# Two more pairs in seven products, one pair fewer, and the differences in a step of their own

## The chip, the cores and the metric

The kernel runs on one core of a Trainium2 chip. The metric is the device time of one execution in microseconds. Before the change the median of three runs is 991.41 us (990.34 to 991.68).

## The reference

One layer of a hybrid decoder trunk, in fp32, for 256 tokens of width 2048:

```python
h = rmsnorm(x, norm_g)
proj = h @ w_in                                   # 2048 -> 13824 columns
qa, ka, va, ga, qb, kb, vb, gb, xc, gc, mg = jnp.split(proj, cuts, axis=-1)
ya = moba_attention(qa, ka, va, rpe_table)        # 8 heads of 128
yb = swa_attention(qb, kb, vb, sinks, rpe_table)  # 16 query heads of 64, window 128
yc = rglru_branch(xc, conv_w, conv_b, w_r, b_r, w_i, b_i, lam)   # conv, two gates in 8 blocks, recurrence
y = jnp.stack([ya * jax.nn.silu(ga), yb * jax.nn.silu(gb), yc * jax.nn.silu(gc)], axis=2)
y_d = jnp.einsum('bsnc,ncd->bsnd', y, w_br)
merged = jnp.einsum('bsnd,bsnd->bsd', jax.nn.sigmoid(mg), y_d)
x = x + merged @ w_out
x = x + jax.nn.sigmoid(rmsnorm(x, ple_norm_g) @ w_pg) * (p @ w_pp)
return rmsnorm(x, final_norm_g)
```

Nearly all of the work is four matrix products with 256 rows: `w_in`, `w_br`, `w_out`, `w_pg`.

## The kernel before

**Precision.** Each fp32 product is three products of rounded parts: hi x hi, hi x lo and lo x hi (`mm3`, matmuls of lines 185, 186 and 187). Activations are split into hi and lo once. Weights are split as they come: a tile of 128 x 1024 (two K tiles of a chunk of 512 columns) is fetched on SP's queue (`fetch`, L110, five buffers, tiles named `r_...`), cast to the hi part on ACT (`split`, L136, `wh_...`), and the lo part is a subtraction on DVE (L138, `wl_...`). Hi and lo have four buffers each, so a cast must wait until TensorE has finished with the tile four places earlier.

**Staging.** A chunk of 512 output columns is 16 K tiles x 2 halves of the tokens x 3 products = 96 matmuls of 128x512, summed in two PSUM banks (`matrix_psum`, two such tiles). Four more banks (`aux`) serve attention, branch C's gate products and the pairs' single products. When a chunk is done ACT evicts it (L657 `to_features` for q, k and gates, two instructions), DVE transposes blocks of it (`flip_...`, L803), and it goes through DRAM to the feature layout.

The chunks of `w_in` are named by their first row: va, xc (16, 24), gc (32, 40), qa (48, 56), ka (64, 72), ga (80, 88), C's merge gates (96 to 120), kv (128), qb (136, 144), gb (152, 160), A's and B's merge gates (168 to 224). Between them stand the tiles of `w_br` (brc, bra, brb). Branch C's eight pairs of gate products `pg0` to `pg7` (matmuls of 128x256) are handed out among the tiles of the q and k chunks. Each one goes round: matmuls, sigmoid of half r on ACT (`rg`, L715), matmuls, sigmoid of half i (`ig`), and casts of the next block's `cv` and `wr` on ACT (L390) with their lo parts on DVE (L391).

**Pairs in seven products.** `pair_of` (L251) takes two chunks together. Their first four K tiles form a 2 x 2 block matrix, multiplied in seven block products in place of eight, with sums and differences of blocks of weights (DVE, L263) and of activations (`make_sums`, L235). A block product is two K tiles x 3 = 6 matmuls of 128x512. Four products (five, one, six, seven: the heads) need nothing of the chunks' PSUM; `head(left)` starts them inside the chunk ahead, one per weight tile near its end. Seven then puts DVE's sums into the PSUM tile of the first chunk, and the plain tiles of the pair add to it. Three, two and four follow between the pair's own tiles. In the kernel before there are pairs for qb (136), the last two merge gates (216), both halves of w_out, and the first two chunks of w_pg. When a pair is opened, three of its four weight blocks are fetched and the difference t1 = 12 - 11 is made at once on DVE; the second difference, 22 - 12, is made in `five`.

**What sets the order.** The program is written once in Python; a scheduler with its own model of the engines orders every engine's instructions when the kernel is built. Each engine then executes its list in that order. `tc.issue_after` and `tc.high_priority` steer it. SP's list holds the fetches of weights in the order of use, each waiting for a free buffer.

## Time and profile before

| | |
|---|---|
| median of three runs | 991.41 us |
| profiled execution | 988.83 us |
| its span | 987.0 us |
| TensorE (PE) busy | 974.9 us, 99%, 4426 matmuls |
| DVE busy | 712.2 us, 72% |
| ACT busy | 587.6 us, 60% |
| DMA | 232.63 MB, mean 236 GB/s |
| granted TensorE clock | 0.997 |

The profiled execution is 1.83 us longer than its span, and 2.58 us shorter than the median. PE is a row of matmuls, PEld its weight loads, which overlap them. A matmul's recorded duration includes its pipeline, so the distance between two starts says what one costs. A time such as "781.48" is the start in microseconds from the begin of the span. Buffer numbers are left out of names in the profile (`wl_in` is the lo part of any tile of w_in).

### The profile page before, as it was taken

To read this page: it belongs to the slowest core of one execution; us is meant where nothing else is said; L and a number is where in the kernel's file an instruction comes from. 1 tells how busy PE (TensorE), PEld (TensorE's weight loads), DVE (VectorE), ACT (ScalarE), POOL (GpSimd) and SP (SyncE) were. 2 spreads that over 40 slices of the span, in tenths; PEclk is the share of its full clock that TensorE was granted. 3 is DMA by queue.
4 is the path that set the end of the run, shared out by engine and by line. 5 is a ranking of instruction groups with operands and counts; after the bars stand their busy time and mean duration, and the time that the engine had idled before them with its cause. 6 is when DMAs were issued, how large, how long until landed. Compare 5 with 4: busy or idle time off the path is not lost.

```text
span 987.0 us, 12481 instructions
## 1 busy us (share of the span) xinstructions
PE 974.9 (99%) x4426; PEld 810.4 (82%) x4426; DVE 712.2 (72%) x1000; ACT 587.6 (60%) x826; POOL 3.6 (0%) x12
## 2 busy tenths in 40 slices
PE   9999999999999999999999999999999999999996
PEld 7888888888888888888888888888888788878886
DVE  6746875566887676666557888698678589898683
ACT  7644645557676566545556767765555455676662
POOL 0000000000000000000000000000000000000000
PEclk9999999999999999999999999999999999999998
DMA  9867876777777767747788776667747967769752
GB/s 360 322 190 226 285 231 222 226 222 236 234 259 246 218 195 246 221 128 232 246 262 267 235 249 218 220 225 230 258 140 258 347 209 261 219 208 360 254 175 85
DMA packets 83494, 232.63 MB, mean 236 GB/s; under 512 B 9400, under 2 KB 30952, under 8 KB 82920
## 3 DMA queue, kind: packets, MB, share of 16 engines
q1 hardware_dynamic: 76896, 219.32, 68.3%
q10 hardware_dynamic: 6536, 12.52, 3.6%
q8 instruction: 34, 0.56, 0.2%
q14 instruction: 28, 0.23, 0.1%
HBM read 211.06 MB, written 20.75 MB: 235 GB/s over the span
## 4 chain that ended last, share of the span: by engine, by line
PE 88%; DVE 4%; DMA 4%; issue 2%; ACT 1%; SPq 0%; DVEq 0%; ACTq 0%
PE ps_in L186 20%; PE ps_in L187 20%; PE ps_in L185 20%; PE ps_pg L185 3%; PE ps_pg L187 3%; PE ps_pg L186 3%; PE ps_bra L186 1%; PE ps_brc L187 1%; PE ps_bra L187 1%; PE ps_bra L185 1%; PE ps_brc L185 1%; PE ps_brc L186 1%; DMA b_out<-w_out_dram 1%; PE ps_brb L187 1%; PE ps_brb L186 1%
## 5 line engine op out<-in xcount | busy, mean ns | idle before, releaser
L138 DVE TENSOR_TENSOR wl_in<-r_in,wh_in 128x1024 fp32r<-128x1024 f32 x224 | 273.0, 1221 | 148.7 <-ACT wh_in L136 143.5
L136 ACT CAST wh_in<-r_in 128x1024 fp32r<-128x1024 f32 x224 | 234.7, 1051 | 203.7 <-PE ps_in L187 163.3
L186 PE MATMUL ps_in<-wl_in,h 128*128 128x512 f32 x896 | 349.3, 390 | 2.1 <-DVE wl_in L138 2.1
L185 PE MATMUL ps_in<-wh_in,h 128*128 128x512 f32 x896 | 349.3, 390 | 0.0
L187 PE MATMUL ps_in<-wh_in,h 128*128 128x512 f32 x896 | 349.0, 390 | 0.0
L186 PEld LDWEIGHTS ps_in<-wl_in,h 128*128 128x128 f32 x896 | 168.3, 188 | 37.1 <-DVE wl_in L138 3.2
L187 PEld LDWEIGHTS ps_in<-wh_in,h 128*128 128x128 f32 x896 | 168.3, 188 | 34.6
L185 PEld LDWEIGHTS ps_in<-wh_in,h 128*128 128x128 f32 x896 | 168.3, 188 | 34.4
L138 DVE TENSOR_TENSOR wl_pg<-r_pg,wh_pg 128x1024 fp32r<-128x1024 f32 x24 | 29.3, 1222 | 14.3 <-ACT wh_pg L136 14.2
L185 PE MATMUL ps_pg<-wh_pg,x_hi 128*128 128x512 f32 (+1 forms) x104 | 38.9, 374 | 0.3 <-DVE ps_pg L263 0.3
L186 PE MATMUL ps_pg<-wl_pg,x_hi 128*128 128x512 f32 (+1 forms) x104 | 38.8, 373 | 0.0
L187 PE MATMUL ps_pg<-wh_pg,x_lo 128*128 128x512 f32 (+1 forms) x104 | 38.8, 373 | 0.0
L186 PE MATMUL ps_out<-wl_out,m_hi 128*128 128x512 f32 x96 | 37.5, 391 | 0.0
L187 PE MATMUL ps_out<-wh_out,m_lo 128*128 128x512 f32 x96 | 37.4, 389 | 0.0
L185 PE MATMUL ps_out<-wh_out,m_hi 128*128 128x512 f32 x96 | 37.2, 390 | 0.0
L136 ACT CAST wh_out<-r_out 128x1024 fp32r<-128x1024 f32 x24 | 25.2, 1052 | 16.8 <-PE ps_out L187 6.5
L136 ACT CAST wh_pg<-r_pg 128x1024 fp32r<-128x1024 f32 x24 | 25.1, 1051 | 13.9 <-PE ps_pg L187 9.8
L138 DVE TENSOR_TENSOR wl_brc<-r_brc,wh_brc 128x1024 fp32r<-128x1024 f32 x16 | 19.6, 1223 | 19.0 <-ACT wh_brc L136 19.0
L136 ACT CAST wh_brc<-r_brc 128x1024 fp32r<-128x1024 f32 x16 | 16.9, 1055 | 25.1 <-PE ps_in L187 25.1
L138 DVE TENSOR_TENSOR wl_out<-r_out,wh_out 128x1024 fp32r<-128x1024 f32 x24 | 29.1, 1217 | 3.3 <-ACT wh_out L136 3.3
L136 ACT CAST wh_brb<-r_brb 128x1024 fp32r<-128x1024 f32 x16 | 16.9, 1054 | 19.6 <-DMA r_brb<-w_br_dram 6.6
L138 DVE TENSOR_TENSOR wl_brb<-r_brb,wh_brb 128x1024 fp32r<-128x1024 f32 x16 | 19.5, 1221 | 8.8 <-ACT wh_brb L136 8.7
(409 smaller groups left out, 1400.7 us busy)
## 6 DMA issues: line engine op xcount, KB each, us to landing
r_in<-w_in_dram SPq DMA_DIRECT2D x228, 512.0 KB, 4.4
r_pg<-w_pg_dram SPq DMA_DIRECT2D x30, 512.0 KB, 4.8
r_out<-w_out_dram SPq DMA_DIRECT2D x28, 512.0 KB, 4.9
r_brc<-w_br_dram SPq DMA_DIRECT2D x16, 512.0 KB, 3.6
r_bra<-w_br_dram SPq DMA_DIRECT2D x16, 512.0 KB, 5.0
r_brb<-w_br_dram SPq DMA_DIRECT2D x16, 512.0 KB, 4.0
d_b<-flip_b SPq DMA_DIRECT2D x32, 96.0 KB, 2.7
turn_b<-d_b SPq DMA_DIRECT2D x8, 384.0 KB, 4.9
```

The lines of the kernel that those rows point to most:

```text
L136: casts.append(nc.scalar.copy(hi[:, c], r[:, c]).ins)
L138: los.append(nc.vector.tensor_tensor(lo[:, c], r[:, c], hi[:, c].bitcast(F32), op=ALU.subtract).ins)
L185: nc.tensor.matmul(ps, ah, bh, start=first, stop=False, **more)
L186: nc.tensor.matmul(ps, ah, bl, start=False, stop=False, **more)
L187: nc.tensor.matmul(ps, al, bh, start=False, stop=last, **more)
```

## The change

1. The two differences of a pair become a step of their own, `differ`, which is the first of now five heads. It stands behind the lo part that was issued last.
2. A pair may be `inside`: products five, one and six use the two banks of its own first PSUM tile, and only seven takes an `aux` bank.
3. Two pairs are added, both `inside`: ka (rows 64 to 79), opened after qa's first chunk, with its heads in qa's second chunk; and gb (152 to 167), opened ahead of the qb pair, with its heads in the second half of the qb pair. The host packs their columns accordingly.
4. The pair of w_pg becomes two plain chunks: K tiles 0 to 11 of both, then 12 to 15 of each. The activation sums of x for that pair go.
5. In branch B's merge, the heads of the next pair start two tiles before the end of chunk 0 or 2 of `w_br` (`beyond`). The sums of the merged activations get a higher priority.

The core of the diff:

```diff
     def head(left):
-        while coming and len(coming) >= left - 1:
+        while coming and len(coming) >= left + beyond[0] - 1:
             coming.pop(0)()
...
-            if alone:
+            if alone and inside and n != 7:
+                if not pss:
+                    pss.append(matrix_psum(f"{name}_0"))
+                dst = pss[0][:, int(n == 5)]
+            elif alone:
                 dst = aux(f"m{n}_{name}")
...
+        def differ():
+            raw["t1"] = temp(f"t1_{name}").rearrange("p k t -> p (k t)")
+            z.update({0: raw["t1"][:, :CW], 1: raw["12"][:, :CW], 2: raw["t1"][:, CW:], 3: raw["12"][:, CW:]})
+            with tc.issue_after(los[-1]):
+                on_vector(raw["t1"], raw["12"], raw["11"], ALU.subtract)
+                on_vector(raw["12"], raw["22"], raw["12"], ALU.subtract)
+
         def five():
-            on_vector(raw["12"], raw["22"], raw["12"], ALU.subtract)
             ms[5] = product(5, sum_of(0), "t1")
...
-        heads = [five, one, six, seven]
+        heads = [differ, five, one, six, seven]
...
-        raw["t1"] = temp(f"t1_{name}").rearrange("p k t -> p (k t)")
-        z.update({0: raw["t1"][:, :CW], 1: raw["12"][:, :CW], 2: raw["t1"][:, CW:], 3: raw["12"][:, CW:]})
-        on_vector(raw["t1"], raw["12"], raw["11"], ALU.subtract)
         return lambda: coming.extend(heads), rest
...
-        for c in range(2):
-            turned_q(c, in_chunk())
+        turned_q(0, in_chunk())
+        open_ka, ka_pair = in_pair(1, True)
+        open_ka()
+        turned_q(1, in_chunk())
...
-        for c in range(2):
-            turned_k(c, in_chunk())
+        ka_pair(turned_k)
...
+        open_gb, gb_pair = in_pair(2, True)
+        open_gb()
         qb_pair(features(qT, rs_q[DB], "qb"))
...
-        for c in range(2):
-            silu(chunk(g, c), f"gb{c}")
+        gb_pair(lambda c, ps: silu(chunk(g, c), f"gb{c}", ps))
...
-            if (bi, n) in ((2, 1), (2, 3)):
-                pairs[0][0]()
+            if bi == 2:
+                beyond[0] = 4 if n % 2 == 0 else 0
+                if n % 2 == 0:
+                    pairs[0][0]()
...
-    pairs.pop(0)[1](KD - 4, gated)
+    pss = [matrix_psum(f"pg{i}").rearrange("p h c -> p (h c)") for i in range(2)]
+    gets = [weights_of(w_pg, i * KD * CW // WT, f"pg{i}", WT // CW) for i in range(2)]
+    for last in (False, True):
+        for i in range(2):
+            for k in range(KD - 4, KD) if last else range(KD - 4):
...
+                    mm3(pss[i][:, h * CW : (h + 1) * CW], [t[:, h * P : (h + 1) * P] for t in act_of(*x2T)[k]],
+                        [t[:, c] for t in w], k == 0, k == KD - 1)
+            if last:
+                gated(i, pss[i].rearrange("p (h c) -> p h c", h=NH))
```

The built order shows it at three places. In names, the number behind the last underscore counts buffers; `in56_7` is weight tile 7 of the chunk at row 56, and `in64_0_6` in a pair is the tile of chunk 0 that starts at K tile 6. Line numbers of the changed kernel are 2 to 23 higher than before (L136 and L138 excepted).

TensorE, where qa's second chunk (in56) ends and ka (in64) begins. Before, pg5's matmuls stand among ka's first tile:

```order
L185 MATMUL ps_in64_1744<-wh_in64_0_1747,h0_109 128x512
L186 MATMUL ps_in64_1744<-wl_in64_0_1748,h0_109 128x512
L185 MATMUL pg5_1372<-cv5_1373,wr5_1376 128x256
L187 MATMUL ps_in64_1744<-wh_in64_0_1747,h0_109 128x512
L185 MATMUL ps_in64_1744<-wh_in64_0_1747,h0_109 128x512
L186 MATMUL pg5_1372<-cv5_1373,wr5_1376 128x256
L187 MATMUL pg5_1372<-cv5_1373,wr5_1376 128x256
L186 MATMUL ps_in64_1744<-wl_in64_0_1748,h0_109 128x512
```

Now in56 is followed by pg5, pg6 (six matmuls each) and one matmul of pg7, and these by product seven, the rest of pg7 and the first plain tile:

```order
L185 MATMUL pg7_1414<-cv7_1415,wr7_1418 128x256
L185 MATMUL m7_in64_1740<-wh_in64_m7_1741,sum_h_824 128x512
L186 MATMUL m7_in64_1740<-wl_in64_m7_1742,sum_h_824 128x512
L187 MATMUL m7_in64_1740<-wh_in64_m7_1741,sum_h_824 128x512
L185 MATMUL m7_in64_1740<-wh_in64_m7_1741,sum_h_824 128x512
L186 MATMUL m7_in64_1740<-wl_in64_m7_1742,sum_h_824 128x512
L187 MATMUL m7_in64_1740<-wh_in64_m7_1741,sum_h_824 128x512
L186 MATMUL pg7_1414<-cv7_1415,wr7_1418 128x256
L187 MATMUL pg7_1414<-cv7_1415,wr7_1418 128x256
L185 MATMUL ps_in64_0_1652<-wh_in64_0_4_1803,h1_110 128x512
```

On ACT at that place now stand the cast of in64_0_6 (its buffer is in56_7's), the evictions of qa's second chunk and the sigmoids and casts of pg5 to pg7 in a row:

```order
L136 CAST wh_in64_0_6_1831<-r_in64_0_6_1829 128x1024
L667 ACTIVATE qa_1431<-ps_in56_1594,rs_q128_575 128x4x128 x2
L725 ACTIVATE rg_587<-pg5_1372,vecs_84 128x256
L269 COPY ps_in64_1_1865<-t1_in64_1631 128x512
L725 ACTIVATE ig_588<-pg5_1372,vecs_84 128x256
L400 CAST cv6_1394<-cv_585 128x256
L400 CAST wr6_1397<-wri_586 128x256
L725 ACTIVATE rg_587<-pg6_1393,vecs_84 128x256
L725 ACTIVATE ig_588<-pg6_1393,vecs_84 128x256
L400 CAST cv7_1415<-cv_585 128x256
L400 CAST wr7_1418<-wri_586 128x256
```

So the gate products stand together where they stood apart.

ACT, where the first chunk of the qb pair (in136_0) ends. Before, four tiles of the second chunk (in136_1) are cast ahead of the evictions of qb:

```order
L136 CAST wh_in136_1_4_3958<-r_in136_1_4_3956 128x1024
L136 CAST wh_in136_1_6_3976<-r_in136_1_6_3974 128x1024
L136 CAST wh_in136_1_8_3994<-r_in136_1_8_3992 128x1024
L136 CAST wh_in136_1_10_4012<-r_in136_1_10_4010 128x1024
L657 ACTIVATE qb_3582<-ps_in136_0_3749,rs_q64_576 128x4x128 x2
L136 CAST wh_in136_1_12_4030<-r_in136_1_12_4028 128x1024
```

Now one is, and behind the evictions they alternate with the products of gb (in152), the first of which is t1:

```order
L136 CAST wh_in136_1_4_3985<-r_in136_1_4_3983 128x1024
L667 ACTIVATE qb_3601<-ps_in136_0_3768,rs_q64_576 128x4x128 x2
L136 CAST wh_in152_m5_4002<-t1_in152_3980 128x1024
L136 CAST wh_in136_1_6_4014<-r_in136_1_6_4012 128x1024
L136 CAST wh_in152_m1_4030<-b_in152_3821 128x1024
L136 CAST wh_in136_1_8_4044<-r_in136_1_8_4042 128x1024
```

On DVE t1 stands behind the flip of qb's first chunk:

```order
L138 TENSOR_TENSOR wl_in136_1_4_3986<-r_in136_1_4_3983,wh_in136_1_4_3985 128x1024
L813 STREAM_TRANSPOSE flip_qb0_3972<-qb_3601 128x8x4x32
L265 TENSOR_TENSOR t1_in152_3980<-b_in152_3821 128x1024
L265 TENSOR_TENSOR b_in152_3821<-r_in152_22_3824,b_in152_3821 128x1024
L138 TENSOR_TENSOR wl_in152_m5_4003<-t1_in152_3980,wh_in152_m5_4002 128x1024
L138 TENSOR_TENSOR wl_in136_1_6_4015<-r_in136_1_6_4012,wh_in136_1_6_4014 128x1024
```

DVE, where the last pair of merge gates (in216) ends and chunk 2 of `w_br` for branch B (brb2) begins. Before, t1 of the out0 pair stands ahead of the last lo part of in216:

```order
L263 TENSOR_TENSOR t1_out0_6594<-b_out0_6589 128x1024
L138 TENSOR_TENSOR wl_in216_1_14_6572<-r_in216_1_14_6569,wh_in216_1_14_6571 128x1024
L263 TENSOR_TENSOR b_out0_6589<-r_out0_22_6592,b_out0_6589 128x1024
L138 TENSOR_TENSOR wl_brb2_0_6600<-r_brb2_0_6597,wh_brb2_0_6599 128x1024
L138 TENSOR_TENSOR wl_brb2_1_6618<-r_brb2_1_6615,wh_brb2_1_6617 128x1024
L138 TENSOR_TENSOR wl_brb2_2_6636<-r_brb2_2_6633,wh_brb2_2_6635 128x1024
```

Now both differences stand behind the lo part of brb2_1:

```order
L138 TENSOR_TENSOR wl_in216_1_14_6610<-r_in216_1_14_6607,wh_in216_1_14_6609 128x1024
L138 TENSOR_TENSOR wl_brb2_0_6636<-r_brb2_0_6633,wh_brb2_0_6635 128x1024
L138 TENSOR_TENSOR wl_brb2_1_6654<-r_brb2_1_6651,wh_brb2_1_6653 128x1024
L265 TENSOR_TENSOR t1_out0_6669<-b_out0_6627 128x1024
L265 TENSOR_TENSOR b_out0_6627<-r_out0_22_6630,b_out0_6627 128x1024
L138 TENSOR_TENSOR wl_brb2_2_6675<-r_brb2_2_6672,wh_brb2_2_6674 128x1024
```

They moved by three lo parts.

## The prediction

> **What bounds the kernel now.** I read the page first: busy times, then the costliest groups.

> ```profile
> span 987.0 us, 12481 instructions
> PE 974.9 (99%) x4426; PEld 810.4 (82%) x4426; DVE 712.2 (72%) x1000; ACT 587.6 (60%) x826; POOL 3.6 (0%) x12
> L138 DVE TENSOR_TENSOR wl_in<-r_in,wh_in 128x1024 fp32r<-128x1024 f32 x224 | 273.0, 1221 | 148.7 <-ACT wh_in L136 143.5
> L136 ACT CAST wh_in<-r_in 128x1024 fp32r<-128x1024 f32 x224 | 234.7, 1051 | 203.7 <-PE ps_in L187 163.3
> L186 PE MATMUL ps_in<-wl_in,h 128*128 128x512 f32 x896 | 349.3, 390 | 2.1 <-DVE wl_in L138 2.1
> ```

> TensorE is busy for nearly the whole span. So time can come from two places only: fewer matmuls, or fewer and shorter waits of TensorE. ACT and DVE have room on average, but their casts and low-part subtractions are released by TensorE itself (ACT waits mostly for `ps_in` L187, the end of an older tile). The splits therefore run only a few tiles ahead.

> Next, the waits of TensorE, all of them:

> ```profile
> PE ps_in L186 <- DVE wl_in L138: 2.1, 2, 1.6
> PE m_pg L185 <- ACT sum_x L247: 0.8, 1, 0.8
> PE busy L452 <- PEq L1262: 0.8, 1, 0.8
> PE ps_pg L185 <- DVE ps_pg L263: 0.3, 1, 0.3
> ```

> Apart from the start, three waits are there to be removed: 1.6 us on a low part of `w_in`, 0.8 and 0.3 us in the w_pg pair. Everything beyond that must come out of the count of matmuls.

> A matmul's recorded 390 ns is not its price, as the starts show:

> ```profile
> 782.51 0.39 PE L187 MATMUL ps_in<-wh_in,h 128*128 128x512 f32 x1
> 782.75 0.39 PE L185 MATMUL ps_in<-wh_in,h 128*128 128x512 f32 x1
> 782.97 0.39 PE L186 MATMUL ps_in<-wl_in,h 128*128 128x512 f32 x1
> ```

> One starts 0.23 us after the other (0.227 over long runs of such rows). That is what a matmul of 128x512 costs here.

> **The change part by part: the matmuls.** A pair saves one of eight block products, 2 K-halves x 3 = 6 matmuls, 6 x 0.227 = 1.36 us. Two pairs are added (ka, gb), one goes (w_pg): net -1.36 us.

> **The w_pg pair's waits.** Both rows above (`m_pg`, `ps_pg`) go with the pair. Recorded idle is 0.83 and 0.30; by starts, which also lose the overlap of 0.16 at the end of an idle piece, it is 0.99 and 0.47. Sum: -1.46. In the new code the K tiles 12 to 15 are asked for only after 144 matmuls of the first two chunks, 144 x 0.227 = 33 us, so I see nothing that takes the place of these waits.

> **The differences of the out0 pair.** The largest wait comes from here:

> ```profile
> 779.06 1.23 DVE L263 TENSOR_TENSOR t_out<-b_out 128x1024 f32<-128x1024 f32 x1 [7.48 <-DMA b_out<-w_out_dram]
> 780.21 1.22 DVE L138 TENSOR_TENSOR wl_in<-r_in,wh_in 128x1024 fp32r<-128x1024 f32 x1
> 781.34 1.22 DVE L263 TENSOR_TENSOR b_out<-r_out,b_out 128x1024 f32<-128x1024 f32 x1
> 782.48 1.22 DVE L138 TENSOR_TENSOR wl_brb<-r_brb,wh_brb 128x1024 fp32r<-128x1024 f32 x1
> 785.34 1.23 DVE L138 TENSOR_TENSOR wl_brb<-r_brb,wh_brb 128x1024 fp32r<-128x1024 f32 x1 [1.65 <-ACT wh_brb L136]
> 781.48 0.50 PE L186 MATMUL ps_in<-wl_in,h 128*128 128x512 f32 x1 [1.58 <-DVE wl_in L138]
> 780.59 1.04 ACT L136 CAST wh_brb<-r_brb 128x1024 fp32r<-128x1024 f32 x1 [2.94 <-DMA r_brb<-w_br_dram]
> 784.26 1.05 ACT L136 CAST wh_brb<-r_brb 128x1024 fp32r<-128x1024 f32 x1 [2.63 <-DMA r_brb<-w_br_dram]
> ```

> DVE stood 7.48 us in front of t1 until the block of w_out landed, with the low part of the last in216 tile queued behind it; TensorE waited 1.74 us by starts (to 781.48). In the new order t1 and the second difference stand behind the low parts of tiles 0 and 1 of brb2. The tile of in216 is freed. But what is late next is in the same fence: ACT waited for the DMA of tile 0 to 780.59 and of tile 1 to 784.26, and neither load changes its place on SP's queue. Tile 1's low part then still ends near 786.6. Had TensorE gone on at 779.74 without a wait, it would ask for this one at 779.74 + 24 x 0.227 = 785.2: it waits 1.4 us there. Behind it on DVE now stand the two differences (2 x 1.14 between starts) before tile 2's low part: that ends at 790.0, asked for at 786.6 + 12 x 0.227 = 789.3, 0.7 us more. Together 2.1 against 1.74 before. I take 0 for this place; the bounds are -1.74 (the loads come earlier too) and +0.7.

> **The ka pair at the end of qa chunk 1 (in56).** Before, TensorE had plain tiles of ka to run while branch C's recurrent-gate products (pg5 to pg7) went back and forth with ACT and DVE:

> ```profile
> 202.51 0.28 PE L185 MATMUL pg<-cv,wr 128*128 128x256 f32 x1
> 202.62 0.28 PE L186 MATMUL pg<-cv,wr 128*128 128x256 f32 x1
> 202.74 0.28 PE L187 MATMUL pg<-cv,wr 128*128 128x256 f32 x1
> 203.06 0.47 ACT L715 ACTIVATE ig<-pg,vecs 128x256 f32<-128x256 f32 x1 [0.67 <-PE pg L187]
> 203.44 0.40 ACT L390 CAST cv<-cv 128x256 fp32r<-128x256 f32 x1
> 203.57 0.42 DVE L718 TENSOR_TENSOR ig<-ig,cv 128x256 f32<-128x256 f32 x1
> 203.73 0.41 ACT L390 CAST wr<-wri 128x256 fp32r<-128x256 f32 x1
> 203.91 0.42 DVE L391 TENSOR_TENSOR cv<-cv,cv 128x256 fp32r<-128x256 f32 x1
> 204.25 0.42 DVE L391 TENSOR_TENSOR wr<-wri,wr 128x256 fp32r<-128x256 f32 x1
> ```

> A step from TensorE's last pg matmul (202.74 + 0.28) to its sigmoid and on to the next split's last subtraction (204.25 + 0.42) takes 1.65 us, and nothing waited since plain tiles lay between. In the built order of the change nothing lies between. Behind in56's last matmul stand pg5, pg6 and the first matmul of pg7, 13 in a row, then product seven (m7), the rest of pg7, and then tile in64_0_4, which adds to a PSUM tile that DVE writes only after m7. Everything is a chain, and it starts late, because ACT has a cast that waits for in56's last matmul and both evictions of qa1 ahead of pg5's sigmoid:

> ```profile
> 195.49 1.05 ACT L136 CAST wh_in<-r_in 128x1024 fp32r<-128x1024 f32 x1 [1.67 <-PE ps_in L187]
> 196.44 1.26 ACT L657 ACTIVATE qa<-ps_in,rs_q 128x512 f32<-128x512 f32 x2
> 197.59 0.47 ACT L715 ACTIVATE rg<-pg,vecs 128x256 f32<-128x256 f32 x1
> ```

> With 0 at the end of in56's last matmul: cast to 1.0, evictions to 2.15 (1.15 between starts), sigmoid of pg5 to 2.62 (197.59 less 195.49 is 2.10, the same chain). pg5's second half starts at 2.66 and ends at 3.18; its sigmoid at 3.22, the splits of pg6 1.61 later (203.06 to 204.67) at 4.83. pg6's last matmul of the first half starts at 4.87, ends 5.15, sigmoid to 5.66, second half 5.70 to 6.22, sigmoid at 6.26; cast of wr7 7.34. pg7's first matmul 7.38, m7 from 7.50, its last matmul starts at 8.63 and ends at 9.02. Then DVE's sum into PSUM:

> ```profile
> L263 DVE TENSOR_TENSOR ps_in<-b_in,m_in x2: 689/692/696, 446.9 to 741.2; 128x512 f32<-128x512 f32 x2
> L263 DVE TENSOR_TENSOR t_in<-b_in x2: 1216/1218/1221, 412.5 to 702.6; 128x1024 f32<-128x1024 f32 x2
> L267 ACT COPY ps_in<-b_in 128x512 f32<-128x512 f32 x4 | 2.3, 586 | 1.4 <-DVE b_in L263 1.4
> ```

> 0.69 from 9.06: tile in64_0_4 starts at about 9.78. TensorE's own work in that time is 15 pg matmuls at 0.117 (202.51 to 202.74 is two) and 6 at 0.227, 3.12 us. **Wait: 6.7 us.** The copy of 0.59 between pg5's two sigmoids and the flip of qa on DVE fit in the chain's own gaps. Bounds: 5.2 if the cast (0.95) and one eviction (0.58) get ahead, 8.0 if the copy (0.59) and half the flip (0.7) fall into the chain.

> **The gb pair at the end of qb chunk 0 (in136).** Here the differences are the new step. On DVE it stands behind the flip of qb0, which needs both evictions, and ACT's next casts stand behind it: first m5 of the gb pair (which is t1), then in136_1_6. Before, four tiles of chunk 1 were cast ahead of the evictions; now one.

> ```profile
> 473.63 1.26 ACT L657 ACTIVATE qb<-ps_in,rs_q 128x512 f32<-128x512 f32 x2
> 474.92 1.25 DVE L803 STREAM_TRANSPOSE flip_qb<-qb 128x1024 f32<-128x1024 f32 x1
> ```

> From in136_0_14's last matmul: evictions to 1.36 (0.1 for the start), flip from 1.4, t1 from 2.58 (starts 1.15 apart, as 780.21 to 781.34) to 3.8, cast of m5 to 4.88, its low part to 6.17. TensorE has tile in136_1_4 (12 matmuls), one of m5 and one of in136_1_6: 14 x 0.227 = 3.18 us, and goes on at 6.2. **Wait: 3.0 us.** Nothing waits behind it: in136_1_6's low part ends at 7.3, when m5's other five matmuls do. Bounds: 1.8 if DVE could take t1 before the flip, 4.0 if a load or another cast comes between.

> **The sum.** 988.83 (profiled execution, 1.83 around the span) - 1.36 - 1.46 + 0 + 6.7 + 3.0 = 995.7. The runs' median, 991.41, lies 2.58 above that execution, so **998.2 us**, 0.7% slower. DVE's extra work for a pair (seven rows of 1.22, three of them low parts of the added products, and four sums of 0.69, some 11 us) I cost at nothing: DVE is 28% idle, and its low parts end 1 to 3 us before they are asked for at the other places; without this cover each would cost up to its length.

> [...] TensorE's clock stayed full across the largest wait of before:

> ```profile
> 780.00:784.00 4.00, 2.52 (x11) 2.10 (x12) 3.69 (x4) 1.04 (x1) 0.00 (x0) 1.00 1.03 410
> ```

> (seventh value, the granted clock: 1.00 with 2.52 of 4 us busy). [...]

> **The rivals.**
> *Neither wait comes.* If pg5 to pg7 get through while TensorE is still busy and t1 is early, the change does what it says: 998.2 - 9.7 = 988.5, or 986.8 with the out0 wait gone as well. For it: the before trace hides exactly these chains at no cost. Against: TensorE takes its matmuls in the order built, and that order has no plain tile there. It decides from the point where the two new waits sum to less than 2.8 us, what is saved elsewhere.
> *One of the two.* Only the ka wait: 995.2. Only the gb wait: 991.5, no change. For it: they are 270 us apart and have different causes.
> *The clock falls.* At half speed for as long after each wait as it lasted (6.7 and 3.0 us), half of that is lost: 4.8 us, 1003. Against: the window row above.

> **How the numbers follow.** Both waits 62%, with its own range 994.5 to 1001; ka's alone 11%; gb's alone 6%; neither 10%; the clock 6%; further waits, where I took DVE's additions as hidden, 5%. About 0.2% (2 us) is what a measurement here can tell from no change. Slower: 62 + 11 + 6 + 5 = 84%. Same: 6%. Faster: 10%. The range, 991 to 1002, leaves out the faster case and the clock, some 2 in 10 at most.

> **What would show it.** In the profile after: a TensorE wait on ACT's sigmoids and casts and on DVE's `cv`/`wr` near 197 to 206 us, summing to 6 to 7 us, in groups named pg; a wait of `ps_in` on the cast and low part of `wl_in_m` near 475 us of about 3 us; no `m_pg` group; near 790 us waits on `wl_brb` in place of `wl_in`. TensorE's count 6 lower and its waits some 10 us larger would make each step right. If pg matmuls alternate with `ps_in` ones near 200 us, the main term is wrong.

## The result

The changed kernel takes 1005.84 us (median of four runs, 1005.45 to 1007.01). The kernel before, run beside it, takes 990.90 us (990.34 to 991.68). The ratio is 1.0148, with a 95% interval of 1.0133 to 1.0164: the change makes the kernel 1.5% slower. The forecast was 998.2 us, slower by 0.7%. The side was right; the size was not, and the time lies outside the range of 991 to 1002.

The profiled executions differ by more than the medians do: 18.2 us of span (1005.2 less 987.0). The one of before was 2.1 us under its median, the one of after (1007.01) 1.2 us above. The account below is made between the two profiled executions.

The page of the changed kernel, its head and the granted clock by slices:

```profile
span 1005.2 us, 12487 instructions
PE 982.8 (98%) x4420; PEld 814.2 (81%) x4420; DVE 720.6 (72%) x1005; ACT 594.9 (59%) x834; POOL 3.2 (0%) x12
PEclk9999999979999999999999999999999999989999
```

The count of matmuls fell by 6, as it should, and TensorE is still busy for 98% of the span. But its busy time rose by 7.9 us. Fewer matmuls can't do that at the same clock, and the granted clock shows a slice at 7 tenths (201 to 226 us) and one at 8 (880 to 905 us).

All waits of TensorE in the changed kernel behind the first 20 us:

```profile
PE ps_out L185 <- ACT wh_out L136: 2.9, 1, 2.9
PE pg L185 <- ACT rg L725: 2.9, 2, 2.4
PE pg L185 <- ACT wr L400: 2.3, 2, 1.2
PE ps_in L185 <- ACT wh_in_m L136: 2.2, 1, 2.2
PE ps_in L185 <- ACT wh_in L136: 0.8, 2, 0.4
PE ps_out L186 <- DVE wl_out L138: 0.5, 1, 0.5
PE ps_in L185 <- DVE ps_in L265: 0.4, 1, 0.4
```

The rows named `pg` and the last one are the ka place, `wh_in_m` is the gb place; both were forecast. Of the two waits in the row `wh_in`, one belongs to the gb place and one stands at 183 us. `wh_out` and `wl_out` were not: they are a third place, in the second half of w_out. The row `m_pg` of before is gone.

The next rows are stretches of 3.41 us of TensorE's time at the three places (columns: length, then busy time of PE, PEld, DVE, ACT and POOL, the granted clock, DMA share, GB/s). Why 3.41 is told in the last section.

```profile
202.03:205.44 3.41, 0.80 (x5) 0.41 (x3) 2.42 (x3) 3.19 (x6) 0.00 (x0) 1.00 0.57 166
205.44:208.85 3.41, 1.94 (x6) 1.50 (x6) 1.67 (x5) 1.33 (x4) 0.00 (x0) 0.50 0.81 270
208.85:212.27 3.42, 2.26 (x6) 1.71 (x6) 1.10 (x3) 1.07 (x3) 0.00 (x0) 0.50 0.34 68
212.27:215.68 3.41, 3.05 (x9) 2.25 (x8) 2.30 (x3) 1.91 (x3) 0.00 (x0) 0.50 0.29 117
485.33:488.75 3.42, 1.26 (x6) 0.65 (x4) 3.38 (x4) 1.39 (x2) 0.00 (x0) 1.00 0.48 110
488.75:492.16 3.41, 3.03 (x8) 2.25 (x8) 3.41 (x4) 2.50 (x3) 0.00 (x0) 0.50 0.53 155
888.11:891.52 3.41, 1.22 (x6) 0.68 (x4) 0.00 (x0) 0.36 (x1) 0.00 (x0) 1.00 1.01 407
891.52:894.93 3.41, 2.20 (x4) 1.45 (x5) 2.69 (x3) 3.11 (x5) 0.00 (x0) 0.50 0.85 300
894.93:898.35 3.42, 3.42 (x9) 2.64 (x8) 3.15 (x4) 3.42 (x10) 0.00 (x0) 0.50 0.84 287
```

At each place TensorE first waits at full clock, and then goes on at half of it for one to three such stretches (at the ka place with more waits in them). At half clock a matmul of 128x512 starts every 0.427 us instead of 0.227.

The rows behind the two waits that were forecast: at the ka place the cast that heads the chain, pg5's second half and the first plain tile; at the gb place t1, its cast and product five.

```profile
201.94 1.04 ACT L136 CAST wh_in<-r_in 128x1024 fp32r<-128x1024 f32 x1 [1.67 <-PE ps_in L187]
204.57 0.38 PE L185 MATMUL pg<-cv,wr 128*128 128x256 f32 x1 [2.36 <-ACT rg L725]
214.13 0.79 PE L185 MATMUL ps_in<-wh_in,h 128*128 128x512 f32 x1 [0.36 <-DVE ps_in L265]
```
```profile
486.08 1.18 DVE L265 TENSOR_TENSOR t_in<-b_in 128x1024 f32<-128x1024 f32 x1
487.36 1.05 ACT L136 CAST wh_in_m<-t_in 128x1024 fp32r<-128x1024 f32 x1 [2.47 <-DVE t_in L265]
488.45 0.57 PE L185 MATMUL ps_in<-wh_in_m,sum_h 128*128 128x512 f32 x1 [2.16 <-ACT wh_in_m L136]
```

The account, from the distances between starts of matmuls ("wait" is what a start with a recorded gap ahead of it lost, "half clock" what the other starts lost):

| term | forecast, us | measured, us |
|---|---|---|
| 6 matmuls fewer | -1.36 | -1.36 |
| waits of the w_pg pair | -1.46 | -1.46 |
| out0 place (near 781 before, near 796 after) | 0 | -1.44 |
| ka place, waits | +6.7 | +6.92 |
| gb place, waits | +3.0 | +3.04 |
| half clock at the ka and gb places | 0 (a rival: 4.8) | 2.85 + 1.37 = +4.22 |
| second half of w_out: waits and half clock | 0 | 4.12 + 2.35, less 0.22 before = +6.25 |
| qa's second chunk, tile of product five (183 us) | 0 | +0.76 |
| other places from 812 to 870 us | 0 | -0.31 |
| start, to the 20th matmul on h (20.79 us before, 22.19 after), and what is left over | 0 | 1.40 + 0.2 = +1.6 |
| sum | +6.9 | +18.2 |

### The profile page after: what moved, and what is told of

The parts are those of the page before. It is cut to its first block, busy times and chain, and to the rows that moved or that the text cites. A ratio compares the mean times of both kernels' runs of the same rounds, so it can differ in the third digit from the quotient of the medians.

```text
span 1005.2 us, 12487 instructions
## 1 busy us (share of the span) xinstructions
PE 982.8 (98%) x4420; PEld 814.2 (81%) x4420; DVE 720.6 (72%) x1005; ACT 594.9 (59%) x834; POOL 3.2 (0%) x12
## 4 chain that ended last, share of the span: by engine, by line
PE 92%; DMA 4%; ACT 1%; DVE 1%; issue 0%; SPq 0%; DVEq 0%; POOL 0%; ACTq 0%
PE ps_in L185 20%; PE ps_in L186 20%; PE ps_in L187 20%; PE ps_pg L187 3%; PE ps_pg L185 3%; PE ps_pg L186 3%; PE ps_out L186 2%; PE ps_out L187 2%; PE ps_out L185 2%; PE ps_bra L186 1%; PE ps_brc L187 1%; PE ps_brc L185 1%; PE ps_bra L187 1%; PE ps_bra L185 1%; PE ps_brc L186 1%; DMA r_out<-w_out_dram 1%
## 5 line engine op out<-in xcount | busy, mean ns | idle before, releaser
L138 DVE TENSOR_TENSOR wl_in<-r_in,wh_in 128x1024 fp32r<-128x1024 f32 x216 | 263.4, 1221 | 126.2 <-ACT wh_in L136 125.0
L185 PE MATMUL ps_in<-wh_in,h 128*128 128x512 f32 x864 | 337.8, 391 | 1.2 <-ACT wh_in L136 0.8
L136 ACT CAST wh_in<-r_in 128x1024 fp32r<-128x1024 f32 x216 | 226.6, 1051 | 187.5 <-PE ps_in L187 151.6
L186 PE MATMUL ps_in<-wl_in,h 128*128 128x512 f32 x864 | 337.0, 390 | 0.2 <-DVE wl_in L138 0.2
L187 PE MATMUL ps_in<-wh_in,h 128*128 128x512 f32 x864 | 336.7, 390 | 0.0
L185 PEld LDWEIGHTS ps_in<-wh_in,h 128*128 128x128 f32 x864 | 162.6, 188 | 35.3 <-ACT wh_in L136 1.5
L186 PEld LDWEIGHTS ps_in<-wl_in,h 128*128 128x128 f32 x864 | 162.4, 188 | 33.7 <-DVE wl_in L138 0.7
L187 PEld LDWEIGHTS ps_in<-wh_in,h 128*128 128x128 f32 x864 | 162.3, 188 | 33.7
L138 DVE TENSOR_TENSOR wl_pg<-r_pg,wh_pg 128x1024 fp32r<-128x1024 f32 x28 | 34.2, 1223 | 24.9 <-ACT wh_pg L136 23.1
L136 ACT CAST wh_pg<-r_pg 128x1024 fp32r<-128x1024 f32 x28 | 29.5, 1052 | 29.0 <-PE ps_pg L187 19.2
L185 PE MATMUL ps_pg<-wh_pg,x_hi 128*128 128x512 f32 (+1 forms) x120 | 45.0, 375 | 0.0
L186 PE MATMUL ps_pg<-wl_pg,x_hi 128*128 128x512 f32 (+1 forms) x120 | 45.0, 375 | 0.0
L187 PE MATMUL ps_pg<-wh_pg,x_lo 128*128 128x512 f32 (+1 forms) x120 | 45.0, 375 | 0.0
L185 PE MATMUL ps_out<-wh_out,m_hi 128*128 128x512 f32 x96 | 38.5, 401 | 2.9 <-ACT wh_out L136 2.9
L136 ACT CAST wh_out<-r_out 128x1024 fp32r<-128x1024 f32 x24 | 25.2, 1052 | 26.6 <-DMA r_out<-w_out_dram 13.5
L138 DVE TENSOR_TENSOR wl_out<-r_out,wh_out 128x1024 fp32r<-128x1024 f32 x24 | 29.1, 1218 | 14.0 <-ACT wh_out L136 14.0
L186 PE MATMUL ps_out<-wl_out,m_hi 128*128 128x512 f32 x96 | 38.5, 401 | 0.5 <-DVE wl_out L138 0.5
L187 PE MATMUL ps_out<-wh_out,m_lo 128*128 128x512 f32 x96 | 38.3, 398 | 0.0
L138 DVE TENSOR_TENSOR wl_brc<-r_brc,wh_brc 128x1024 fp32r<-128x1024 f32 x16 | 19.6, 1222 | 20.2 <-ACT wh_brc L136 18.7
L136 ACT CAST wh_brc<-r_brc 128x1024 fp32r<-128x1024 f32 x16 | 16.9, 1055 | 25.1 <-PE ps_in L187 25.1
L136 ACT CAST wh_brb<-r_brb 128x1024 fp32r<-128x1024 f32 x16 | 16.9, 1054 | 24.4 <-DMA r_brb<-w_br_dram 10.3
L138 DVE TENSOR_TENSOR wl_brb<-r_brb,wh_brb 128x1024 fp32r<-128x1024 f32 x16 | 19.3, 1219 | 13.1 <-ACT wh_brb L136 13.1
```

The source lines that it names most:

```text
L136: casts.append(nc.scalar.copy(hi[:, c], r[:, c]).ins)
L138: los.append(nc.vector.tensor_tensor(lo[:, c], r[:, c], hi[:, c].bitcast(F32), op=ALU.subtract).ins)
L185: nc.tensor.matmul(ps, ah, bh, start=first, stop=False, **more)
L186: nc.tensor.matmul(ps, ah, bl, start=False, stop=False, **more)
L187: nc.tensor.matmul(ps, al, bh, start=False, stop=last, **more)
```

## The experiments

### Each new piece undone alone, and all three

Four kernels, each the changed one with something undone. In e1 ka is two plain chunks again:

```diff
-        open_ka, ka_pair = in_pair(1, True)
-        open_ka()
         turned_q(1, in_chunk())
...
-        ka_pair(turned_k)
+        for c in range(2):
+            turned_k(c, in_chunk())
```

> The changed kernel with ka as two plain chunks again (all else kept). Theory: three separate places lost the time, and each can be read from TensorE's starts in the changed kernel: some 9.7 us at the ka pair (gate products in a row, the half clock behind them included), 4.4 at the gb pair, 6.3 at out2. Then this kernel is 9.7 - 1.36 (the pair's saving) = 8.3 us faster than the change, about 997.5 us, the pg matmuls alternate with plain tiles near 200 us, and the two other places stay. Rival: the loss is one common thing (a later start of everything, loads that run later), and the wait moves to the next place: then less than 4 us come back.

In e2 the same is done to gb:

```diff
-        open_gb, gb_pair = in_pair(2, True)
-        open_gb()
...
-        gb_pair(lambda c, ps: silu(chunk(g, c), f"gb{c}", ps))
+        for c in range(2):
+            silu(chunk(g, c), f"gb{c}")
```

> The changed kernel with gb as two plain chunks again. Theory of separate places: 4.4 - 1.36 = 3.0 us faster than the change, about 1002.8 us, with the ka and out2 places as they were. Rival (waits move): no more than 1 us.

In e3 the two loads of p @ w_pp's result (`pp`) and the load of `fg`, 1 MB each on ACT's queue, are asked for three steps later:

```diff
-    for h in range(2):
-        nc.scalar.dma_start(pps[h], pp_d[h])
-
     fg = block("fg")
-    nc.scalar.dma_start(fg[:, :D], bass.AP(tensor=fin.tensor, ...))
+
+    def last_loads():
+        for h in range(2):
+            nc.scalar.dma_start(pps[h], pp_d[h])
+        nc.scalar.dma_start(fg[:, :D], bass.AP(tensor=fin.tensor, ...))
+
+    later(3, last_loads)
```

> The changed kernel with ACT's three loads of 1 MB (pp, twice, and the final norm's gain) issued three weight tiles after the last one of w_out, where the kernel before had them; nothing else. Theory: in the changed kernel they went out at 877 to 878 us, 16 us earlier than before, since the buffers that the w_pg pair held are free, and the r_out loads behind them took 12.8 us to land; without them the wait at out2 (6.3 us with its half clock) goes: about 999.5 us. Rival: the r_out loads are late because SP's queue stood behind turn_x21 until 877.8; then the wait stays and the time is within 1 us of the change.

In e4 all three are done:

> The changed kernel without the ka pair, without the gb pair, and with the late loads: what is left of the change is the step of differences of its own, the earlier heads in branch B's merge and w_pg in plain chunks. Theory of separate places: 1005.8 - 8.3 - 3.0 - 6.3 = 988.2 us, 2.7 us under the kernel before, and no TensorE wait over 0.7 us is left. Rival (the wait near 781 us only moves to brb2, as the prediction had it): 990 to 991.

| | median, us | ratio to before | 95% interval |
|---|---|---|---|
| changed kernel | 1005.84 | 1.0148 | 1.0133 to 1.0164 |
| e1, no ka pair | 997.24 | 1.0053 | 1.0038 to 1.0068 |
| e2, no gb pair | 1003.50 | 1.0107 | 1.0066 to 1.0149 |
| e3, late loads | 1001.02 | 1.0081 | 1.0048 to 1.0115 |
| e4, all three | 987.39 | 0.9959 | 0.9943 to 0.9976 |

e1, e2 and e4 came out as expected, within 1 us. In e1 the matmuls of pg5 to pg7 stand among plain tiles again, and from 195 to 225 us TensorE loses nothing; the gb place and w_out are as in the changed kernel. In e4 nothing is lost between 20 and 950 us, and what is left of the change is 0.4% faster than before.

e3 shows what the third place was. In the changed kernel ACT issued the three loads at 877 us, ahead of SP's five fetches of w_out. These are ACT's issues and the first cast behind them, then TensorE:

```profile
877.14 0.82 ACTq L1106 DMA_DIRECT2D pp<-pp_d  x2
877.99 0.44 ACTq L1109 DMA_DIRECT2D fg<-fin_dram  x1
891.16 2.16 ACT L136 CAST wh_out<-r_out 128x1024 fp32r<-128x1024 f32 x2 [10.26 <-DMA r_out<-w_out_dram]
```
```profile
892.26 0.79 PE L185 MATMUL ps_out<-wh_out,m_hi 128*128 128x512 f32 x1 [2.93 <-ACT wh_out L136]
893.52 0.79 PE L186 MATMUL ps_out<-wl_out,m_hi 128*128 128x512 f32 x1 [0.47 <-DVE wl_out L138]
```

And the DMAs issued from 876 to 897 us (KB of one, then median us from issue to landing):

```profile
r_out<-w_out_dram SPq DMA_DIRECT2D x5, 512.0 KB, 13.5
pp<-pp_d ACTq DMA_DIRECT2D x2, 1024.0 KB, 4.7
fg<-fin_dram ACTq DMA_DIRECT2D x1, 1024.0 KB, 12.9
```

Over the whole execution the page has for the same fetch:

```profile
r_out<-w_out_dram SPq DMA_DIRECT2D x28, 512.0 KB, 5.0
```

A fetch of w_out that takes 5.0 us in the median took 13.5 here, with the DMA engines full (share 1.01, 407 GB/s in the stretch from 888 us). The 3 MB that nobody needs yet went ahead of the 2.5 MB that TensorE was about to ask for. Before the change the same loads went out later:

```profile
893.78 0.82 ACTq L1094 DMA_DIRECT2D pp<-pp_d  x2
894.75 0.53 ACTq L1097 DMA_DIRECT2D fg<-fin_dram  x1
```

In e3 they go out at 903 us, and between 870 and 912 us TensorE loses nothing (6.47 in the changed kernel). That the early loads cause this loss is thereby shown. Why the scheduler put them earlier is read from the code: `pp` and `fg` live in the pool of wide blocks (L65), of which the w_pg pair of before had taken one for its sums (`sum_x`, L236 there) and one for its weights (`b_pg`, L350 there). Without the pair two are free. e9 below, which brings the pair back and leaves the loads' code alone, agrees: they go out at 899 us.

e3 gained less than expected, since 2.0 us came back near 797 us as waits of `ps_brb` on `wl_brb`. That is the wait forecast for the out0 place. It goes with the time at which SP issues the second fetch of that chunk of w_br: 5.0 us ahead of the chunk's first matmul in e3, 6.3 in e5 (loss 1.7), 10.7 in the changed kernel (0.4) and 11.2 in e4 (none). What decides this on SP's queue was not settled.

### Why m7 waits for pg5 to pg7

The forecast read from the built order that m7 stands behind pg7's first matmul, but not why. Two theories: ACT and DVE are late with pg5 to pg7 whatever stands around them; or the pool of four `aux` banks hands them out in turn, so that m7, asked for behind pg5 to pg7, gets the bank behind theirs. e5 gives m7 of ka a bank of its own (three for the others):

```diff
     def aux(name):
-        return ps_x.tile([P, CW], F32, tag="aux", name=name)
+        return ps_x.tile([P, CW], F32, tag="aux", name=name, bufs=3)
...
-                dst = aux(f"m{n}_{name}")
+                dst = ps_x.tile([P, CW], F32, tag="seven", name=f"m{n}_{name}", bufs=1) if name == "in64" else aux(f"m{n}_{name}")
```

> The changed kernel, where product seven of the ka pair has a PSUM bank of its own (the pool of four aux banks is split in three and one); nothing else. Theory: m7 stood behind pg7's first matmul because both ask for banks of one pool that hands them out in turn, and every plain tile of ka waits for m7's sum. With a bank of its own m7 is built into in56's tile 5, ka's plain tiles follow in56 at once and pg5 to pg7 stand among them: the 9.7 us at the ka pair go, about 996 us (attention with three banks in place of four may cost some of it). Rival: the chain of gate products and the evictions are what is late, whoever has the bank: 1004 us or more.

e6 starts ka's heads two tiles earlier:

```diff
+        beyond[0] = -2
         turned_q(1, in_chunk())
+        beyond[0] = 0
```

> The changed kernel with the heads of the ka pair two weight tiles earlier in in56. In the built order pg5 and half of pg6 are then done before in56 ends, and the second half of pg6, the first matmul of pg7 and m7 remain behind it. Theory (the wait is the length of the chain that is left): cast and evictions 2.2, sigmoid, three matmuls, sigmoid and splits to pg7 2.7, m7 and the sum 2.2, less 2.2 us of TensorE's own work: 4.5 us and about 1.3 of half clock in place of 9.7, so some 4 us faster than the change, 1002 us. Rival (the place does not depend on the gate products): within 1 us of the change.

e5: 996.59 us, ratio 1.0036 (1.0021 to 1.0052), as expected, and between 190 and 225 us TensorE waits for nothing. In its built order m7's first matmul stands behind product six in in56's tiles 4 and 5, and pg5 to pg7 lie among ka's plain tiles. The steps of the gate chain on ACT take as long as in the changed kernel (sigmoid 0.47 us, casts 0.39 to 0.41); the chain is only no longer between m7 and these tiles. So it was the turn of the banks.

e6: 1006.56 us, ratio 1.0139 (1.0113 to 1.0165), where 1002 was expected. TensorE's starts behind a gap, from 172 to 212 us:

```profile
177.90 0.39 PE L185 MATMUL pg<-cv,wr 128*128 128x256 f32 x1 [1.16 <-ACT wr L400]
179.24 0.39 PE L186 MATMUL pg<-cv,wr 128*128 128x256 f32 x1 [0.95 <-DVE cv L401]
180.93 0.50 PE L185 MATMUL ps_in<-wh_in,h 128*128 128x512 f32 x1 [0.44 <-ACT wh_in L136]
181.84 0.62 PE L186 MATMUL ps_in<-wl_in_m,sum_h 128*128 128x512 f32 x1 [0.42 <-DVE wl_in_m L138]
...
211.24 0.39 PE L185 MATMUL pg<-cv,wr 128*128 128x256 f32 x1 [2.76 <-ACT wr L400]
```

The old place shrank from 6.92 to 3.64 us, but pg4's chain now stands ahead of product five and costs 4.23 there, and 1.92 at half clock. Earlier heads moved the wait instead of removing it. The clock fell there too, at 182.07 us, though none of these pauses is longer than 1.16 us.

### A kernel in which both pairs are kept

e7 takes ga for a pair in place of ka (branch C's gate products are done by then), starts gb's heads one tile earlier, and has the late loads of e3:

```diff
-        ka_pair(turned_k)
-        for c in range(2):
-            silu(chunk(g, c), f"ga{c}")
+        turned_k(0, in_chunk())
+        open_ga, ga_pair = in_pair(1, True)
+        open_ga()
+        turned_k(1, in_chunk())
+        ga_pair(lambda c, ps: silu(chunk(g, c), f"ga{c}", ps))
...
+        beyond[0] = -1
         qb_pair(features(qT, rs_q[DB], "qb"))
+        beyond[0] = 0
```

> Two pairs are kept but placed where nothing stands in their way: ga (rows 80 to 95) in place of ka, opened after ka's first chunk, when the gate products are through; gb with its heads one tile earlier, so that DVE makes t1 before the flip of qb0; and the late loads as in e3. Theory: none of the three waits is left and the two pairs save 2 x 1.36 us on top of e4: 987.4 - 2.7 = 984.7 us. Rival: DVE's extra work for two pairs (some 11 us each) makes new waits in the stages that run close: 986 us or more.

987.22 us, ratio 0.9947 (0.9931 to 0.9963); 984.7 was expected. The gb place is free of waits. New ones of 2.54 us stand at the ga pair's heads. DVE there:

```profile
220.81 1.25 DVE L813 STREAM_TRANSPOSE flip_ka<-ka 128x1024 f32<-128x1024 f32 x1 [1.71 <-ACT ka L667]
226.99 1.22 DVE L265 TENSOR_TENSOR t_in<-b_in 128x1024 f32<-128x1024 f32 x1 [4.67 <-DMA d_ka<-flip_ka]
```

t1 takes one of the four `temp` buffers, and by the trace's releaser had to wait until the flip of ka had gone out to DRAM. e10 starts the ga heads one tile later:

```diff
+        beyond[0] = 1
         turned_k(1, in_chunk())
+        beyond[0] = 0
```

> e7 with the heads of the ga pair one weight tile later in in72. In e7 TensorE waited 2.54 us near 229 to 237 us for m5 and a low part behind it: t1 took a buffer that the flip of ka still needed until its DMA landed at 227 us. One tile is 2.7 us. Theory: that wait goes, so 2.5 us less than e7, 984.7 us, and both pairs' 2.7 us show against e12. Rival: DVE's work for the pair is too much for this stage, and the wait only moves: within 0.7 us of e7.

987.15 us, ratio 0.9957 (0.9941 to 0.9973), again not 984.7. The waits at the heads are gone; in their place the first plain tile of ga waits for seven's sum into PSUM:

```profile
249.65 0.50 PE L185 MATMUL ps_in<-wh_in,h 128*128 128x512 f32 x1 [1.77 <-DVE ps_in L265]
```

It loses 1.93 us there by starts, and 0.11 behind it. The heads' first place is too early and one tile later too late; an order in between was not tried. e11 therefore leaves the first branch alone: gb's pair, its heads one tile earlier, late loads, no pair for ka or ga. Beside it e4's kernel ran again (e12).

> The gb pair alone, with its heads one tile earlier, no ka or ga pair, and the late loads. Theory: no wait at its place, so 1.36 us less than e12: 986 us. Rival: the DVE work shows up later as a wait, and the time is that of e12 or above.

> The kernel of e4 on the same chip as e9 to e11, as their reference: 987.4 us, 4 us under the kernel before.

e11: 986.20 us, ratio 0.9945 (0.9932 to 0.9957). e12: 987.02, ratio 0.9960 (0.9944 to 0.9975). The intervals of their ratios overlap, so the difference of the two is read from the trace: from the 20th matmul on h to TensorE's last one e11 takes 953.75 us, e12 955.15, which is 1.40 less. The pair's six matmuls are 1.36. All that TensorE waits for in e11:

```profile
PE ps_pp L511 <- ACT whi_pp L509: 1.2, 1, 1.2
PE busy L462 <- PEq L1289: 0.8, 1, 0.8
PE ps_in L186 <- DVE wl_in L138: 0.4, 1, 0.4
```

All three lie in the first 20 us. e11 has the lowest median of all kernels run; it is 5.5 us under the kernel before that ran beside it. By their ratios (0.9945 and 0.9947, on different chips) it and e7 cannot be told apart.

### The w_pg pair kept, with the differences in their own step

Was it worth removing the w_pg pair, for 1.36 us of matmuls and 1.46 of waits? e9 is the changed kernel with ka and gb plain and the w_pg pair as before, opened with `differ` like the others:

```diff
-    pairs.pop(0)[1](KD, lambda i, ps: residual(2 + i, ps))
+    pairs.append(pair_of(lambda: act_of(*x2T), lambda: sums["x2"], w_pg, 0, "pg0"))
+    out_pair = pairs.pop(0)
+    pairs[0][0]()
+    out_pair[1](KD, lambda i, ps: residual(2 + i, ps))
...
-    pss = [matrix_psum(f"pg{i}").rearrange("p h c -> p (h c)") for i in range(2)]
...
+    pairs.pop(0)[1](KD - 4, gated)
```

> The kernel before with the step of differences of its own and the earlier heads in branch B's merge only: neither ka nor gb as a pair, and the w_pg pair with its sums kept. Theory: the wait near 781 us (1.74) goes as in e4, the two of the w_pg pair (1.46) stay: about 1.7 us under the kernel before, and about 0.1 us above e4, since the pair's saving of 1.36 and its waits of 1.46 cancel. Rival: the w_pg pair is what cost, and this kernel is no faster than before.

995.17 us, ratio 1.0034 (1.0022 to 1.0047): slower than before, where 1.7 us less was expected. DVE, then TensorE in e9:

```profile
877.43 1.22 DVE L1086 TENSOR_TENSOR xr<-ps_out,xr 128x1024 f32<-128x1024 f32 x1
878.68 1.31 DVE L813 STREAM_TRANSPOSE flip_x<-xr 128x512 f32<-128x512 f32 x2
880.11 1.22 DVE L265 TENSOR_TENSOR t_pg<-b_pg 128x1024 f32<-128x1024 f32 x1
```
```profile
882.52 0.79 PE L185 MATMUL m_pg<-wh_pg_m,sum_x 128*128 128x512 f32 x1 [5.79 <-ACT wh_pg_m L136]
```

In its own step t1 stands behind the residual of the finished chunk and its flips, and product five waits for it: 6.92 us of waits and 2.47 at half clock between 870 and 912 us. It is the gb place again (there one flip stands ahead of t1). So the step `differ` and the w_pg pair, as the code stands, do not go together, and making w_pg plain belongs to the change.

### How long a wait lowers the clock

The waits at the gb place are 2.16 and 0.38 us, and behind the first the granted clock fell to 0.50; behind the largest wait of before, 1.58 us, it stayed at 1.00. e8 is the kernel before with a forced pause of TensorE in each of five chunks (in8 to in40): small matmuls into an `aux` bank, one to eight copies on ACT, and a matmul that waits for them.

```diff
+    probes = {"in8": 1, "in16": 2, "in24": 3, "in32": 5, "in40": 8}
+
+    def probe(n):
...
+            for _ in range(n):
+                nc.scalar.copy(t, pt)
+            nc.scalar.copy(pt[:, :P], t[:, :P])
+            return nc.tensor.matmul(pt[:, :P], one, one, start=True, stop=True).ins
```

> The kernel before, in which TensorE is made to stand idle once in each of five chunks of w_in (in8, in16, in24, in32, in40) by a chain of ACT copies between two small matmuls: idle pieces of about 1.3, 1.9, 2.5, 3.6 and one of 7 us that is broken by gate products. It computes the same. Theory: the half clock behind the waits comes from idleness alone, with a threshold between 1.6 us (the wait of the kernel before, clock 1.00) and 2.2 us (gb pair, clock halved): matmuls 0.227 us apart after the first piece and 0.427 apart for some 3 us after the longer ones. [...] Rival: the clock falls with the work after the wait, not the wait, and stays full here.

One execution: 1020.92 us, granted clock 0.989. The pauses with 1, 2 and 3 copies (1.56, 1.65 and 2.31 us) left the granted clock at 1.00; the one with 5 (3.54 us) lowered it to 0.50 and cost 2.54 us behind it. The fifth was broken up by branch C's gate matmuls; the clock fell to 0.50 there too, and 2.97 us were lost. The first and the fourth:

```profile
53.64 0.49 PE L202 MATMUL probe<-const-float32-1.0 128*128 128x128 f32 x2 [1.56 <-ACT probe L201]
53.88 0.48 PE L185 MATMUL ps_in<-wh_in,h 128*128 128x512 f32 x1
```
```profile
131.03 0.80 PE L202 MATMUL probe<-const-float32-1.0 128*128 128x128 f32 x2 [3.54 <-ACT probe L201]
131.47 0.77 PE L185 MATMUL ps_in<-wh_in,h 128*128 128x512 f32 x1
```

The theory of a limit near 2 us for one piece of idle time falls with the piece of 2.31. What replaces it is in the last section.

## Why the prediction was right and wrong

**Right.** The four terms that were read from the trace came out to within 0.25 us: the matmuls (-1.36), the w_pg pair's waits (-1.46), the ka place (6.7 forecast, 6.92 measured) and the gb place (3.0 and 3.04). So the way to the two large ones holds: take the built order, find what stands between two matmuls on the other engines, and add the durations of before. For the ka place e1 shows the pair as the cause and e5 the mechanism, the bank. For the gb place e2 shows the pair, and e11, in which t1 is asked for one tile earlier, the place of t1.

The rows show how far the ka chain went as forecast. Counted from the start of the cast at 201.94, pg5's second half starts at 2.63 us (2.66 forecast). Then the clock falls, and the first plain tile starts at 12.19 instead of 9.78. The waits alone still add up to the forecast, because what half clock added is a term of its own here.

**Wrong: "I see nothing that takes the place of these waits."** This was said of the w_pg pair's removal, and considered matmuls only. With the pair two wide blocks became free (by the code, as said above), and three loads of 1 MB moved up by 17 us into the fetches of w_out: +6.25 us, the largest error. The order on ACT shows it: the loads of `pp` stand ahead of the last seven casts of w_out, where before they stood behind a cast of w_pg. The work that hid those fetches was priced at nothing without asking what else would be in flight.

**Wrong: the clock as a rival of 6%.** It happened at all three places. That waits such as these let the clock fall to half was the author's assumption then; the rows above show it, 0.50 in the stretches behind them. The sum counted each wait once; ka and gb paid it nearly one and a half times (9.96 us of waits, 4.22 behind them at half clock). The rival's own price, 4.8 us, was near, in part by luck: it let half clock last as long as the wait, 6.7 us at the ka place. There it lasted 10.24 us (205.44 to 215.68), and TensorE stood idle for part of that. The argument against it was the row of 780 us with 2.52 of 4 us busy. That was too weak: matmuls worth 1.82 us at full clock start in the stretch of 3.41 us there (779.79 to 783.21), and 0.91 or less in those ahead of the three falls. At w_out, which the forecast did not have, half clock took another 2.35 us.

**Wrong by 1.4 us: the out0 place at 0.** Both differences moved behind the low parts as forecast, but the loads came earlier too (SP issued the second fetch of that chunk of w_br 10.7 us ahead of the chunk's first matmul, where it was 6.3 before), which was the lower bound given (-1.74). In e3 and e5 the wait on `wl_brb` that was forecast came, with 2.0 and 1.7 us.

**DVE's added work** cost nothing at other places, as assumed: TensorE lost nothing between 222 and 475 and between 500 and 770 us. Only at 183 us, beside product five of the ka pair, a tile of in56 was cast late, which cost 0.76.

**Not foreseen, and nothing ties it to the change:** 1.6 us, of which 1.40 stand ahead of the 20th matmul on h. That start varies by 1.7 us between the executions of all these kernels (20.7 to 22.4 us). The forecast terms as measured (+7.1), half clock at the first two places (+4.2) and w_out (+6.25) with out0 (-1.4) and the small rest (+2.0) make the 18.2. Between the medians the forecast missed by 7.6 us (1005.84 against 998.2), between the profiled executions by 11.3 (18.2 against 6.9).

## What to carry to other kernels

When a change frees a buffer, list what was waiting for one, and what will be in flight when that starts earlier: here three loads of 1 MB went out 17 us earlier, and the fetches behind them took 13.5 us, where the median of the run is 5.0. Where a rotating pool hands out banks, look for who asked ahead, needed or not: at the ka place m7 stood behind pg5 to pg7, and in e5 a bank of its own took 6.92 us of waiting to nothing. Price a wait of TensorE with little work around it above its length: the ka, gb and w_out places waited 6.92, 3.04 and 4.12 us and lost another 2.85, 1.37 and 2.35 at half clock, while a pause of 2.31 us in e8 and one of 2.76 in e6 left the clock at 1.00.

## What the runs showed of the hardware

What goes with a fall is little work in the stretch ahead. Count the matmuls that start in it, each at its full-speed distance (0.227 us for 512 columns, in proportion for fewer). From 22 us on, 31 stretches at full clock in the 14 traces had 1.14 us of such work or less, a third of 3.41 (17 inside the kernels and 14 at their ends); the next was at half clock each time. In every one with 1.19 or more the clock stayed. At half clock, stretches with up to 1.25 stayed there, those with 1.59 or more led back to full speed, and with 1.36 it went both ways. So a pause of 2 to 3 us cost nothing more in e8 (2.31) and e6 (2.76), but 1.37 us of half clock at the gb place (2.16) and 2.35 in w_out (2.93), by where the grid cut it. In e6 a pause of 2.76 us (the last row of its fence above) is cut at 209.38 into 0.90 and 1.86, and the clock stays at 1.00:

```profile
205.97:209.38 3.41, 2.50 (x14) 1.79 (x12) 1.87 (x3) 1.85 (x4) 0.00 (x0) 1.00 0.64 205
209.38:212.79 3.41, 1.55 (x7) 1.35 (x8) 3.10 (x5) 2.30 (x6) 0.00 (x0) 1.00 0.54 205
212.79:216.20 3.41, 2.85 (x13) 2.18 (x13) 2.68 (x4) 1.97 (x3) 0.00 (x0) 1.00 0.63 189
```

In the changed kernel the pause of 2.16 at the gb place lies whole in one stretch (485.33 to 488.75, four starts: 0.91), and the clock falls to 0.50. The probe agrees: 2.31 us were cut into 0.76 and 1.55, which left 1.70 of work in the poorer stretch, and the clock stayed at 1.00; 3.54 left one stretch with 0.34, and it fell to 0.50. So does e6, where pauses of 0.95, 0.44 and 0.42 us leave 0.91 of work between 178.66 and 182.07, and the next stretch is at half clock:

```profile
182.07:185.49 3.42, 3.42 (x9) 2.65 (x9) 3.42 (x5) 1.07 (x2) 0.00 (x0) 0.50 0.49 145
```

So the length of a single pause does not decide it: the clock fell at pauses of 2.16 and 2.93 us, and at 182.07 us in e6 with none above 0.95 in the stretch ahead, and it stayed at pauses of 2.31 and 2.76. The limit between 1.14 and 1.19 us of work is drawn from these traces after the fact; no run was made to test it.

**A fetch behind early loads.** Five fetches of 512 KB were issued with 3 MB of other loads just ahead of the first. The four of them whose landing the trace has took 8.6 to 14.3 us, where the median of the run is 5.0. In e3, with these loads later, the median of the same five is 7.4.
